# Two of the four weight sums of a seven-product matrix pair, added by DMAs that accumulate

## The chip, the cores and the metric

The kernel runs on one core of one Trainium2 chip. The metric is the device time of one execution in microseconds (us). The core has five instruction queues that work in parallel, each strictly in its own order: TensorE (PE in the profile; its weight loads are the row PEld), VectorE (DVE), ScalarE (ACT), GpSimd (POOL) and SyncE (SP, which here only issues DMAs). They wait for one another through semaphores. Sixteen DMA engines move data between the chip's memory (HBM) and the on-chip buffer (SBUF). A DMA can be issued from SP, as all weight loads of this kernel are, or from POOL.

## The reference

One transformer block on 512 tokens of width 1024: two kinds of attention, an output projection, and a gated feed-forward part of width 2816 with a short causal convolution, then a gated per-layer embedding. The change touches the first half of the feed-forward part alone:

```python
h = rmsnorm(x, mlp_pre_g[i])
gu = h @ w_gate_up[i]                  # [512, 1024] @ [1024, 2 * 2816]
a, u = jnp.split(gu, [D_FF], axis=-1)
a = causal_dwconv(a, conv_w[i], conv_b[i])
y = (gelu(a, approximate=True) * u) @ w_down[i]
```

All numbers are float32, and the kernel keeps that precision: each operand of a matmul is split into a high part, in the narrower format that TensorE takes at full rate (float32r), and a low part, the rest. One product is then three matmuls: high by high, low by high, high by low.

## The kernel before, in words

The 2816 columns of `a` and of `u` are cut into 22 tiles of 128. A *pair* j is tile j of `a` and tile j of `u`. Its weights come as two tiles of 128 partitions by 1024 numbers (512 KB each): `m[0]` (called `wr` in the profile, two buffers) for `a`, and `m[1]` for `u`. The 1024 numbers are the contraction's 8 chunks of 128 columns; `W` = 512 is half of them.

Pairs 0 to 8 are computed plainly. Pairs 9 to 21 (`SEVEN = range(9, NFF)`, 13 pairs) are computed as a product of 2 by 2 blocks in seven products in place of eight, in the manner of Strassen and Winograd. The blocks are the halves of the weights on one side, and on the other the halves of the contraction by the two halves of 256 tokens. This costs sums ahead of the products and behind them:

- `token_sums` makes sums and differences of the activations once, before the first such pair (`b` the blocks, `t` their four sums, all on DVE).
- `sums` makes four sums of the weights' halves for each pair, on DVE, 128x512 each. `s13` holds two of them: its left half is `m1[:, :W] + m1[:, W:]` (L1048), its right half `m0[:, :W] - m1[:, :W]` (L1056). `s24` holds the two that build on it (L1052, L1054).
- `high` and `low` split three operands of 128x1024 for each pair: `m0`, `s24` and `s13`. `high` is a copy on ACT (L1038), `low` a subtraction on DVE (L1042). `last_high` and `last_low` (L1060, L1064) do it for the right half of `m1`, 128x512.
- `product(j, n)` is 12 matmuls with 256 moving columns (lines L1080, L1083, L1084: four chunks, three matmuls each). Products 0 and 2 use the split `m0`, products 1 and 6 `s24`, 3 and 4 `s13`, 5 the right half of `m1`. A pair uses three PSUM banks `p[0]` to `p[2]`: products 0, 1, 3, 5 add up in `p[0]`, product 2 has `p[1]`, and 4 and 6 add up in `p[2]`.
- `evict(j, n)` takes what is in a bank out after product n, before the next product adds to it: n = 0, 1, 3 on ACT (L1091, L1094), n = 2, 4, 6 on DVE (L1096, L1098, L1100).
- `conv(j, n)` is the convolution and gelu (ACT L1114, DVE L1116 twice, ACT L1119); `finish` multiplies by `u` (DVE L1127 twice; L1129 for a plain pair).

The order of all this is written out by hand: `up_rest` puts each step into a list with a time (`at(t, f)`), sorts the list, and calls the steps; `keep` holds the instructions in that order on their engines. TensorE works two pairs interleaved: the products come in the order (j,0), (j-1,6), (j,1), (j,2), (j,3), (j,4), (j,5), (j+1,0), and so on. While TensorE multiplies for pair j, DVE and ACT prepare pair j+1. Between two instructions L1098 DVE therefore does, in this order: the four sums of the next pair but one, its `low` of `m0` and `last_low`, L1100, `low` of `s24`, L1116 twice, L1096, `low` of `s13`, L1127 twice, and the next L1098.

Buffers rotate by tag; what takes a buffer waits until the last reader of its former tenant is done. Tag `pt` has three: they hold `s13` and the low part of `s13` of the pairs in flight. Before the change the two tenants move round all three.

Of the kernel before, what the change touches and what calls it, by code (L numbers as in the profile page):

```python
# [8 lines left out]
F32 = mybir.dt.float32  # L9
F32R = mybir.dt.float32r  # L10
I32 = mybir.dt.int32
AF = mybir.ActivationFunctionType
ALU = mybir.AluOpType

P = 128
# [51 lines left out]
class Block:  # L67
# [909 lines left out]
    def token_sums(self):  # L977
# [6 lines left out]
        for p in range(Q):  # L984
# [7 lines left out]
            nc.vector.tensor_sub(t[:, 0:2, :], b[:, 1:4:2, :], b[:, 0:2, :])  # L992
            nc.vector.tensor_sub(t[:, 2, :], b[:, 3, :], t[:, 0, :])
            nc.vector.tensor_sub(t[:, 3, :], b[:, 2, :], t[:, 2, :])
# [11 lines left out]
    def up_rest(self, pending):  # L1006
# [20 lines left out]

        def load(j):
            w[j] = x = {"m": []}
            for i in range(2):  # L1030
                t = self.u([P, D], F32, "tt") if i else self.wrp.tile([P, D], F32, tag="wr", name=self.nm("wr"))
                keep(nc.sync.dma_start(t, io["gu"][2 * j + i]))
                x["m"].append(t)
# [10 lines left out]
        def sums(j, n):  # L1044
            m0, m1 = w[j]["m"]
            if n == 0:
                w[j]["s13"] = self.u([P, D], F32, "pt")
                keep(add(w[j]["s13"][:, :W], m1[:, :W], m1[:, W:]))  # L1048
            s13 = w[j]["s13"]
            if n == 1:  # L1050
                w[j]["s24"] = self.u([P, D], F32, "tt")
                keep(sub(w[j]["s24"][:, :W], s13[:, :W], m0[:, :W]))  # L1052
            if n == 2:
                keep(sub(w[j]["s24"][:, W:], m0[:, W:], w[j]["s24"][:, :W]))  # L1054
            if n == 3:
                keep(sub(s13[:, W:], m0[:, :W], m1[:, :W]))  # L1056

        def last_high(j):
            w[j]["x"] = x = self.u([P, 2, W], F32R, "wh")
            keep(act.activation(x[:, 0, :], w[j]["m"][1][:, W:], AF.Copy))  # L1060

        def last_low(j):
            x = w[j]["x"]
            keep(sub(x[:, 1, :], w[j]["m"][1][:, W:], x[:, 0, :].bitcast(F32)))  # L1064
# [56 lines left out]
        def finish(j):  # L1121
            z = st[j]
            y = self.y_room(j)
            if j in SEVEN:
                for i, u in enumerate((z["p"][0], z["e"][:, 1, :])):
                    t = slice(i * H, i * H + H)
                    keep(vec.tensor_mul(y[:, t], z["c"][:, t], u))  # L1127
# [13 lines left out]
        for j in js:  # L1141
            b = start[j] - (10.5 if j == NPLAIN else start[j] - start[j - 1])
            t = start[j]
            at(b - 7.0, lambda j=j: load(j))
            st[j] = {"p": []}
            if j in SEVEN:
                at(b - 1.0, lambda j=j: sums(j, 0))
                at(b - 0.4, lambda j=j: sums(j, 1))
                at(b + 0.2, lambda j=j: sums(j, 2))
                at(b + 0.8, lambda j=j: sums(j, 3))  # L1150
# [245 lines left out]
```

## Time and profile before

| | |
|---|---|
| Time, 3 runs | 665.62 us median (665.56 to 667.8) |
| Profiled execution | 668.27 us, of which the instructions span 666.5 us |
| Granted TensorE clock | 0.999 |
| PE busy over the span | 652.6 us (98%) |
| PEld busy | 565.5 us (85%) |
| DVE busy | 480.7 us (72%) |
| ACT busy | 363.1 us (54%) |
| POOL busy | 147.4 us (22%) |

The 1.8 us between span and time lie around the instructions. The shares are means over stages of different kinds. The seven-product pairs are the stage from about 362 us to 500 us after the span's start (the names `strassen_...`), where DVE and PE are both busy nearly all the time and POOL is idle. A row of the timeline gives an instruction's start, its duration, engine, line, operation and operands, and in brackets how long its engine had been idle before it and who ended that. The shown duration of a DVE or ACT instruction overlaps the next by about 0.1 us; from start to start is what it takes out of its queue. Rows with `x2` merge two like instructions. Of a DMA issue, the page gives the median time from issue to landing.

### The profile page before, as it was taken

The page shows a single profiled execution, that of the slowest core. Times are in us where ns is not written, and L with a number is a line of the kernel's source. Part 1 is how long each engine was busy: PE and PEld are TensorE (multiplying, and loading weights), DVE is VectorE, ACT ScalarE, POOL GpSimd, SP SyncE. Part 2 cuts the span into 40 slices and gives each one's busy share as a digit, 9 for nine tenths or more (in the row PEclk, how much of TensorE's full clock was granted, in tenths as well). Part 3 has the DMA queues.
Part 4 walks back from the last instruction along what each step waited for, and adds up shares of the span by engine and source line. Part 5 has one row for each costly group of instructions (what it writes and reads, how often), then busy time and mean ns, then how long its engine had stood idle before and what let it go on. Part 6 is the DMA issues. An engine that isn't in the chain of part 4 may idle for free.

```text
span 666.5 us, 10339 instructions
## 1 busy us (share of the span) xinstructions
PE 652.6 (98%) x3741; PEld 565.5 (85%) x3741; DVE 480.7 (72%) x965; ACT 363.1 (54%) x684; POOL 147.4 (22%) x223
## 2 busy tenths in 40 slices
PE   8999999999999999999999999999999999999996
PEld 7988768777888777888887999999998888889985
DVE  6795777878757757858999999999958333224872
ACT  6554688878868737445555565565736323222351
POOL 1021568558556241003221000000000000001000
PEclk9999999999999999999999999999999999999999
DMA  8346721111121557412241332332244554332031
GB/s 299 115 139 213 199 64 47 34 48 49 48 73 56 179 206 269 173 57 95 95 160 63 127 109 83 128 117 76 95 144 156 153 209 143 88 111 71 1 127 63
DMA packets 27282, 78.01 MB, mean 117 GB/s; under 512 B 3424, under 2 KB 4704, under 8 KB 27232
## 3 DMA queue, kind: packets, MB, share of 16 engines
q1 hardware_dynamic: 27088, 77.28, 35.6%
q8 instruction: 29, 0.48, 0.3%
q14 instruction: 21, 0.17, 0.1%
q10 hardware_dynamic: 144, 0.08, 0.0%
HBM read 63.72 MB, written 6.29 MB: 105 GB/s over the span
## 4 chain that ended last, share of the span: by engine, by line
PE 79%; DVE 11%; ACT 4%; DMA 2%; issue 2%; POOL 1%; ACTq 0%; DVEq 0%
PE nsa_pso L548 3%; PE mlpdown_pss L147 3%; PE mlpdown_pss L150 3%; PE mlpdown_pss L151 3%; PE strassen_pss L1080 3%; PE strassen_pss L1084 2%; PE strassen_pss L1083 2%; PE nsa_pst L515 2%; PE mlpdown_psmm L147 2%; PE mlpdown_psmm L150 2%; PE mlpdown_psmm L151 2%; DMA outproj_wr<-in_wo_dram 2%; PE strassen_pst L1080 2%; PE strassen_pst L1083 2%; PE strassen_pst L1084 2%
## 5 line engine op out<-in xcount | busy, mean ns | idle before, releaser
L132 DVE TENSOR_TENSOR mlpdown_wh<-mlpdown_wr,mlpdown_wh 128x1024 fp32r<-128x1024 f32 (+1 forms) x28 | 32.3, 1158 | 48.6 <-ACT mlpdown_wh L128 47.6
L128 ACT ACTIVATE mlpdown_wh<-mlpdown_wr 128x1024 fp32r<-128x1024 f32 (+1 forms) x28 | 27.9, 998 | 63.5 <-PE mlpdown_pss L150 25.9
L237 POOL TENSOR_TENSOR mlpdown_s<-mlpdown_s,mlpdown_s 128x512 f32<-128x512 f32 x6 | 7.8, 1292 | 238.1 <-ACT mlpdown_s L236 238.1
L537 POOL TENSOR_SCALAR nsa_u<-nsa_u,nsa_nrc,gate 128x512 f32<-128x512 f32 (+3 forms) x64 | 38.2, 607 | 22.5 <-DVE nsa_nrc L662 16.7
L1080 PE MATMUL strassen_pss<-sums_u,strassen_u 128*128 128x256 f32 x144 | 40.6, 282 | 1.6 <-ACT strassen_s L1091 1.6
L1084 PE MATMUL strassen_pss<-sums_u,strassen_u 128*128 128x256 f32 x144 | 40.5, 281 | 0.0
L1083 PE MATMUL strassen_pss<-sums_u,strassen_u 128*128 128x256 f32 x144 | 40.5, 281 | 0.0
L631 ACT ACTIVATE nsa_u<-nsa_u,nsa_nnm 128x512 f32<-128x512 f32 (+3 forms) x64 | 35.4, 555 | 5.3 <-DVE nsa_nnm L627 5.0
L519 DVE TENSOR_TENSOR nsa_u<-nsa_pst,nsa_u 128x512 fp32r<-128x512 f32 (+1 forms) x43 | 29.0, 684 | 9.1 <-ACT nsa_u L517 8.8
L627 DVE CUSTOM_DVE_ANT_0 nsa_u<-nsa_pss,biastables_u 128x512 f32<-128x512 f32 (+3 forms) x64 | 29.9, 485 | 5.4 <-PE nsa_pss L569 5.0
L1042 DVE TENSOR_TENSOR strassen_u<-strassen_u,strassen_u 128x1024 fp32r<-128x1024 f32 x27 | 33.3, 1237 | 0.0
L517 ACT ACTIVATE nsa_u<-nsa_pst 128x512 fp32r<-128x512 f32 (+1 forms) x43 | 25.1, 591 | 13.2 <-PE nsa_pst L515 12.8
L147 PE MATMUL mlpdown_pss<-mlpup_u,mlpdown_wh 128*128 128x512 f32 (+1 forms) x88 | 32.0, 364 | 0.0
L150 PE MATMUL mlpdown_pss<-mlpup_u,mlpdown_wh 128*128 128x512 f32 (+1 forms) x88 | 32.0, 364 | 0.0
L151 PE MATMUL mlpdown_pss<-mlpup_u,mlpdown_wh 128*128 128x512 f32 (+1 forms) x88 | 32.0, 363 | 0.0
L132 POOL TENSOR_TENSOR fill_wh<-fill_wr,fill_wh 128x512 fp32r<-128x512 f32 (+1 forms) x14 | 24.7, 1762 | 33.0 <-ACT fill_wh L128 32.9
L1038 ACT ACTIVATE strassen_u<-strassen_u 128x1024 fp32r<-128x1024 f32 x27 | 28.4, 1051 | 1.2 <-DVE strassen_u L1054 1.1
L1080 PEld LDWEIGHTS strassen_pss<-sums_u,strassen_u 128*128 128x128 f32 x144 | 27.3, 190 | 1.9 <-ACT strassen_s L1091 1.8
L548 PE MATMUL nsa_pso<-nsa_u,vnatural_u 128*128 128x512 f32 x72 | 27.2, 441 | 0.9 <-ACT nsa_u L517 0.3
L1083 PEld LDWEIGHTS strassen_pss<-sums_u,strassen_u 128*128 128x128 f32 x144 | 27.2, 189 | 0.1
L1084 PEld LDWEIGHTS strassen_pss<-sums_u,strassen_u 128*128 128x128 f32 x144 | 27.2, 189 | 0.0
L1083 PE MATMUL strassen_pst<-sums_u,strassen_u 128*128 128x256 f32 x88 | 24.8, 282 | 0.0
(502 smaller groups left out, 2302.9 us busy)
## 6 DMA issues: line engine op xcount, KB each, us to landing
mlpdown_wr<-in_down_dram SPq DMA_DIRECT2D x16, 512.0 KB, 3.6
strassen_wr<-in_gu_dram SPq DMA_DIRECT2D x14, 512.0 KB, 4.6
strassen_u<-in_gu_dram SPq DMA_DIRECT2D x14, 512.0 KB, 3.9
mlpup_wr<-in_gu_dram SPq DMA_DIRECT2D x10, 512.0 KB, 3.3
fill_wr<-in_win_dram SPq DMA_DIRECT2D x6, 512.0 KB, 3.8
mlpdown_wr<-in_down_dram SPq DMA_DIRECT2D x8, 384.0 KB, 3.2
fill_u<-fill_u SPq DMA_DIRECT2D x20, 128.0 KB, 2.5
loadx_u<-in_xT_dram SPq DMA_DIRECT2D x8, 256.0 KB, 4.7
```

What stands on the lines that cost most here:

```text
L132: l = eng.tensor_sub(lw, raw, hi.bitcast(F32))
L147: r = self.pin(mm(ps, hi, x[:, 0, :], start=start, stop=False))
L150: mm(ps, lo, x[:, 0, :], start=False, stop=False)
L151: mm(ps, hi, x[:, 1, :], start=False, stop=stop)
L537: self.nc.gpsimd.tensor_scalar(ap, ap, col, gate, op0=ALU.mult, op1=ALU.mult)
L548: self.att(nc.tensor.matmul(po, v, rhs, start=start, stop=stop))
L627: nc.vector.tensor_tensor_reduce(dst, src, dist, op0=ALU.add, op1=ALU.min, scale=SLOPES[8 + 4 * g + r], scalar=3e38, accum_out=nm[:, r, b ...
L631: nc.scalar.activation(dst, dst, AF.Exp, bias=nm[:, r, b : b + 1], scale=-1.0, accum_out=sm[:, r, b : b + 1])
L1042: keep(sub(lo, src, hi.bitcast(F32)))
L1080: r = mm(ps, hi[:, o], x[:, 0, :], start=fresh and p == 0, stop=False, skip_group_check=not fresh)
L1083: mm(ps, lo[:, o], x[:, 0, :], start=False, stop=False, skip_group_check=not fresh)
L1084: mm(ps, hi[:, o], x[:, 1, :], start=False, stop=p == Q - 1, skip_group_check=not fresh)
```

## The change

The sums in `s13` are made by DMAs. `load_sums(j)`, called 1.0 planned units ahead of `load(j)`, has SP load the left half of `m0` into the right half of `s13`, and the right half of `m1` into its left half. Then POOL issues one DMA that reads the left half of `m1` from HBM twice and adds it to both halves of `s13` in SBUF (`accum_op=ALU.add`). The left half of `m1` is no longer loaded by `load`, so `m[1]` of such a pair is 128x512.

A DMA can add but not subtract, so the signs move: the right half of `s13` is now `m0[:, :W] + m1[:, :W]`, the token sums `t` are formed with other signs (two of their four subtractions become scalar_tensor_tensor with a factor of -1), and `finish` multiplies by -1 as well (L1132, scalar_tensor_tensor in place of tensor_tensor). DVE's `sums` keeps two of its four instructions. The change is described as also treating one pair more in this way (14 of 22). The line `SEVEN = range(9, NFF)` stands in both kernels, though: 13 pairs before, 13 after.

```diff
@@ token_sums
-            nc.vector.tensor_sub(t[:, 0:2, :], b[:, 1:4:2, :], b[:, 0:2, :])
-            nc.vector.tensor_sub(t[:, 2, :], b[:, 3, :], t[:, 0, :])
-            nc.vector.tensor_sub(t[:, 3, :], b[:, 2, :], t[:, 2, :])
+            nc.vector.tensor_sub(t[:, 0:2, :], b[:, 0:4:3, :], b[:, 1:2, :].broadcast_to([P, 2, H]))
+            nc.vector.scalar_tensor_tensor(t[:, 2, :], b[:, 3, :], -1.0, t[:, 0, :], op0=ALU.mult, op1=ALU.subtract)
+            nc.vector.scalar_tensor_tensor(t[:, 3, :], t[:, 2, :], -1.0, b[:, 2, :], op0=ALU.mult, op1=ALU.subtract)
@@ up_rest
+        def load_sums(j):
+            w[j] = x = {}
+            x["s13"] = self.u([P, D], F32, "pt")
+            keep(nc.sync.dma_start(x["s13"][:, W:], io["gu"][2 * j][:, :W]))
+            keep(nc.sync.dma_start(x["s13"][:, :W], io["gu"][2 * j + 1][:, W:]))
+            keep(nc.gpsimd.dma_start(x["s13"].rearrange("p (b w) -> p b w", b=2),
+                                     io["gu"][2 * j + 1][:, None, :W].broadcast_to([P, 2, W]), accum_op=ALU.add))
+
         def load(j):
-            w[j] = x = {"m": []}
+            x = w.setdefault(j, {})
+            x["m"] = []
             for i in range(2):
                 t = self.u([P, D], F32, "tt") if i else self.wrp.tile([P, D], F32, tag="wr", name=self.nm("wr"))
-                keep(nc.sync.dma_start(t, io["gu"][2 * j + i]))
+                if i and j in SEVEN:
+                    t = t[:, W:]
+                keep(nc.sync.dma_start(t, io["gu"][2 * j + i][:, -t.shape[1] :]))
                 x["m"].append(t)
...
         def sums(j, n):
-            m0, m1 = w[j]["m"]
+            m0, s13 = w[j]["m"][0], w[j]["s13"]
             if n == 0:
-                w[j]["s13"] = self.u([P, D], F32, "pt")
-                keep(add(w[j]["s13"][:, :W], m1[:, :W], m1[:, W:]))
-            s13 = w[j]["s13"]
+                w[j]["s24"] = self.u([P, D], F32, "tt")
+                keep(add(w[j]["s24"][:, :W], s13[:, :W], m0[:, :W]))
             if n == 1:
-                w[j]["s24"] = self.u([P, D], F32, "tt")
-                keep(sub(w[j]["s24"][:, :W], s13[:, :W], m0[:, :W]))
-            if n == 2:
-                keep(sub(w[j]["s24"][:, W:], m0[:, W:], w[j]["s24"][:, :W]))
-            if n == 3:
-                keep(sub(s13[:, W:], m0[:, :W], m1[:, :W]))
+                keep(add(w[j]["s24"][:, W:], w[j]["s24"][:, :W], m0[:, W:]))
...
-                    keep(vec.tensor_mul(y[:, t], z["c"][:, t], u))
+                    keep(vec.scalar_tensor_tensor(y[:, t], u, -1.0, z["c"][:, t], op0=ALU.mult, op1=ALU.mult))
...
+            if j in SEVEN:
+                at(b - 8.0, lambda j=j: load_sums(j))
             at(b - 7.0, lambda j=j: load(j))
             st[j] = {"p": []}
             if j in SEVEN:
-                at(b - 1.0, lambda j=j: sums(j, 0))
-                at(b - 0.4, lambda j=j: sums(j, 1))
-                at(b + 0.2, lambda j=j: sums(j, 2))
-                at(b + 0.8, lambda j=j: sums(j, 3))
+                at(b + 0.2, lambda j=j: sums(j, 0))
+                at(b + 0.8, lambda j=j: sums(j, 1))
```

The orders of PE and ACT are the same before and after, instruction for instruction. From here on a line number above L1027 belongs to the kernel that the sentence speaks of; the new lines are L1033 (the accumulating DMA), L1031 and L1032 (its two loads), L1043 (`load`), L1053 (`low`), L1059 and L1061 (the two sums left), L1069 (`last_low`), L1101, L1103, L1105 (evictions 2, 4, 6), L1121 (convolution) and L1132 (`finish`).

On DVE, one pair's round before, from `low` of `s13` of one pair to the convolution. In brackets stand the queues that an instruction waits for: the engines' semaphores, `DMAHW` for DMAs of SP.

```order
L1042 TENSOR_TENSOR strassen_u_4212<-strassen_u_4133,strassen_u_4211 128x1024 [waits Activation_49]
L1127 TENSOR_TENSOR strassen_u_4117<-strassen_s_4194,strassen_pso_4009 128x256 [waits Activation_49]
L1127 TENSOR_TENSOR strassen_u_4117<-strassen_s_4194,strassen_s_4042 128x256
L1098 TENSOR_TENSOR strassen_s_4170<-strassen_s_4170,strassen_pss_4231 128x256 [waits PE_49,Activation_49]
L1048 TENSOR_TENSOR strassen_u_4260<-strassen_u_4192 128x512 [waits DMAHW5_49]
L1052 TENSOR_TENSOR strassen_u_4262<-strassen_u_4260,strassen_wr_4190 128x512 [waits DMAHW4_49,DVE_49]
L1054 TENSOR_TENSOR strassen_u_4262<-strassen_wr_4190,strassen_u_4262 128x512 [waits DVE_49]
L1056 TENSOR_TENSOR strassen_u_4260<-strassen_wr_4190,strassen_u_4192 128x512
L1042 TENSOR_TENSOR strassen_u_4279<-strassen_wr_4190,strassen_u_4278 128x1024 [waits Activation_49]
L1064 TENSOR_TENSOR strassen_u_4298<-strassen_u_4192,strassen_u_4298 128x512 [waits PE_49,Activation_49]
L1100 TENSOR_TENSOR mlpup_u_3149<-strassen_s_4170,strassen_pss_4231 128x256 [waits PE_49]
```

The same stretch now; `DMASW` stands for DMAs of POOL.

```order
L1053 TENSOR_TENSOR strassen_u_4220<-strassen_u_4048,strassen_u_4219 128x1024 [waits DMAHW0_49,PE_49,Activation_49]
L1132 SCALAR_TENSOR_TENSOR strassen_u_4124<-strassen_pso_4011,strassen_s_4202 128x256 [waits Activation_49]
L1132 SCALAR_TENSOR_TENSOR strassen_u_4124<-strassen_s_4045,strassen_s_4202 128x256
L1103 TENSOR_TENSOR strassen_s_4174<-strassen_s_4174,strassen_pss_4239 128x256 [waits PE_49,Activation_49]
L1059 TENSOR_TENSOR strassen_u_4281<-strassen_u_4177,strassen_wr_4198 128x512 [waits DMAHW6_49,DMAHW5_49,DMASW4_49]
L1061 TENSOR_TENSOR strassen_u_4281<-strassen_u_4281,strassen_wr_4198 128x512 [waits DVE_49]
L1053 TENSOR_TENSOR strassen_u_4284<-strassen_wr_4198,strassen_u_4283 128x1024 [waits Activation_49]
L1069 TENSOR_TENSOR strassen_u_4303<-strassen_u_4200,strassen_u_4303 128x512 [waits DMAHW7_49,PE_49,Activation_49]
L1105 TENSOR_TENSOR mlpup_u_3149<-strassen_s_4174,strassen_pss_4239 128x256 [waits PE_49]
```

Two instructions are gone, the first of the sums left waits for POOL's DMA, and `low` of `s13` (the first row) has got a wait for PE. It comes from the buffers: `s13` is now claimed a pair earlier, so that two of the three `pt` buffers always hold an `s13`, and every low part of `s13` is written to the third. That one is free when TensorE has read the former pair's low part for the last time, at the second-last matmul of product 4, the last but one of the matmuls that L1103 waits for.

On SP, the DMAs of the stage before: two of 512 KB for each pair, its `wr` (`m[0]`) and its `u` (`m[1]`). A `u` waits for DVE's `last_low` of the pair before, and with it the `wr` behind it.

```order
L1032 DMA strassen_u_4192<-in_gu_dram 128x1024 [waits DMAHW3_49,DVE_49]
L1032 DMA strassen_wr_4317<-in_gu_dram 128x1024 [waits DMAHW2_49]
L1032 DMA strassen_u_4319<-in_gu_dram 128x1024 [waits DMAHW5_49,DVE_49]
L1032 DMA strassen_wr_4445<-in_gu_dram 128x1024 [waits DMAHW4_49]
L1032 DMA strassen_u_4447<-in_gu_dram 128x1024 [waits DMAHW7_49,DVE_49]
```

And now: the two halves of `s13` (L1031, L1032) ahead of each `wr`. The wait for DVE of L1031 is for `low` of `s13` of the pair two before, whose buffer it takes.

```order
L1043 DMA strassen_u_4200<-in_gu_dram 128x512 [waits DMAHW3_49,DVE_49]
L1031 DMA strassen_u_4305<-in_gu_dram 128x512 [waits DMAHW0_49,DMAHW1_49,DMASW3_49,DVE_49]
L1032 DMA strassen_u_4305<-in_gu_dram 128x512
L1043 DMA strassen_wr_4326<-in_gu_dram 128x1024 [waits DMAHW2_49]
L1043 DMA strassen_u_4328<-in_gu_dram 128x512 [waits DMAHW7_49,DVE_49]
```

On POOL, which had one multiplication of this stage and then nothing until the next stage, the 13 accumulating DMAs now stand; here the first of them, among POOL's last work of the stage before.

```order
L974 TENSOR_TENSOR mlpup_s_3605<-mlpup_s_3605,r3b 128x512
L974 TENSOR_TENSOR mlpup_s_3695<-mlpup_s_3695,r3b 128x512
L1033 DMA strassen_u_3798<-in_gu_dram 128x2x512
L1144 TENSOR_TENSOR strassen_s_3811<-strassen_s_3811,r3b 128x512
L1033 DMA strassen_u_3858<-in_gu_dram 128x2x512
L1033 DMA strassen_u_3940<-in_gu_dram 128x2x512
```

The first accumulating DMA stands behind both L974 and ahead of the multiplication L1144, for which a `finish` on DVE waits; each of the DMAs waits for its two loads.

More of the change, by code (lines that the diff above doesn't have):

```diff
@@ L1044, in sums @@
         def sums(j, n):
-            m0, m1 = w[j]["m"]
+            m0, s13 = w[j]["m"][0], w[j]["s13"]
             if n == 0:
-                w[j]["s13"] = self.u([P, D], F32, "pt")
-                keep(add(w[j]["s13"][:, :W], m1[:, :W], m1[:, W:]))
-            s13 = w[j]["s13"]
+                w[j]["s24"] = self.u([P, D], F32, "tt")
+                keep(add(w[j]["s24"][:, :W], s13[:, :W], m0[:, :W]))
             if n == 1:
-                w[j]["s24"] = self.u([P, D], F32, "tt")
-                keep(sub(w[j]["s24"][:, :W], s13[:, :W], m0[:, :W]))
-            if n == 2:
-                keep(sub(w[j]["s24"][:, W:], m0[:, W:], w[j]["s24"][:, :W]))
-            if n == 3:
-                keep(sub(s13[:, W:], m0[:, :W], m1[:, :W]))
+                keep(add(w[j]["s24"][:, W:], w[j]["s24"][:, :W], m0[:, W:]))
         def last_high(j):
             w[j]["x"] = x = self.u([P, 2, W], F32R, "wh")
-            keep(act.activation(x[:, 0, :], w[j]["m"][1][:, W:], AF.Copy))
+            keep(act.activation(x[:, 0, :], w[j]["m"][1], AF.Copy))
         def last_low(j):
             x = w[j]["x"]
-            keep(sub(x[:, 1, :], w[j]["m"][1][:, W:], x[:, 0, :].bitcast(F32)))
+            keep(sub(x[:, 1, :], w[j]["m"][1], x[:, 0, :].bitcast(F32)))
         def product(j, n):
```

## The prediction, made before the changed kernel was run

> **What bounds the kernel now.** I read the page's busy times first, then the stages, then the waits of TensorE (PE) in the stage that is changed. The first line is from the page. The next three are busy time by stage (span, then each engine's busy time and instructions, granted clock, DMA share, GB/s), and the last is all that PE waited for between 300 and 480 us.
>
> ```profile
> PE 652.6 (98%) x3741; PEld 565.5 (85%) x3741; DVE 480.7 (72%) x965; ACT 363.1 (54%) x684; POOL 147.4 (22%) x223
> core 0: us, PE busy (x) PEld busy (x) DVE busy (x) ACT busy (x) POOL busy (x), PEclk, DMA share, GB/s
> 300.00:350.00 50.00, 50.00 (x222) 41.42 (x222) 45.27 (x66) 27.48 (x39) 13.98 (x7) 1.00 0.34 116
> 362.30:480.00 117.70, 116.06 (x977) 115.82 (x977) 114.95 (x176) 70.18 (x108) 0.00 (x0) 1.00 0.32 109
> PE strassen_pss L1080 <- ACT strassen_s L1091: 1.6, 1, 1.6
> ```
>
> In the stage, DVE is busy for 114.95 of 117.70 us, which looks like a bound. PE is busier still: 116.06, and it waited once, for 1.6 us, at the start. So no more than 1.6 us, a quarter of a percent, can come out of the waits here, however much DVE is relieved. PE sets the pace: 977 matmuls in 116.06 us are 0.1188 us each, 84 a pair, 9.98 us a pair.
>
> The next rows are DVE's timeline over one pair in the steady part; then PE's two last matmuls of a product 4 and the first of the product 3 that follows five products later; then two rows of ACT.
>
> ```profile
> 409.50 1.22 DVE L1042 TENSOR_TENSOR strassen_u<-strassen_u,strassen_u 128x1024 fp32r<-128x1024 f32 x1
> 410.64 0.41 DVE L1127 TENSOR_TENSOR strassen_u<-strassen_s,strassen_psmm 128x256 f32<-128x256 f32 x1
> 410.97 0.42 DVE L1127 TENSOR_TENSOR strassen_u<-strassen_s,strassen_s 128x256 f32<-128x256 f32 x1
> 411.45 0.42 DVE L1098 TENSOR_TENSOR strassen_s<-strassen_s,strassen_pss 128x256 f32<-128x256 f32 x1
> 411.79 0.68 DVE L1048 TENSOR_TENSOR strassen_u<-strassen_u 128x512 f32<-128x512 f32 x1
> 412.51 0.69 DVE L1052 TENSOR_TENSOR strassen_u<-strassen_u,strassen_wr 128x512 f32<-128x512 f32 x1
> 413.24 0.69 DVE L1054 TENSOR_TENSOR strassen_u<-strassen_wr,strassen_u 128x512 f32<-128x512 f32 x1
> 413.85 0.68 DVE L1056 TENSOR_TENSOR strassen_u<-strassen_wr,strassen_u 128x512 f32<-128x512 f32 x1
> 414.45 1.22 DVE L1042 TENSOR_TENSOR strassen_u<-strassen_wr,strassen_u 128x1024 fp32r<-128x1024 f32 x1
> 415.58 0.68 DVE L1064 TENSOR_TENSOR strassen_u<-strassen_u,strassen_u 128x512 fp32r<-128x512 f32 x1
> 416.19 0.41 DVE L1100 TENSOR_TENSOR mlpup_u<-strassen_s,strassen_pss 128x256 f32<-128x256 f32 x1
> 421.41 0.42 DVE L1098 TENSOR_TENSOR strassen_s<-strassen_s,strassen_psmm 128x256 f32<-128x256 f32 x1
> ...
> 410.95 0.28 PE L1083 MATMUL strassen_pss<-sums_u,strassen_u 128*128 128x256 f32 x1
> 411.07 0.28 PE L1084 MATMUL strassen_pss<-sums_u,strassen_u 128*128 128x256 f32 x1
> ...
> 418.30 0.28 PE L1080 MATMUL strassen_psmm<-sums_u,strassen_u 128*128 128x256 f32 x1
> ...
> 416.63 0.82 ACT L1114 ACTIVATE strassen_s<-mlpup_u,cols 128x512 f32<-128x512 f32 x1 [0.47 <-DVE mlpup_u L1100]
> 417.36 0.36 ACT L1094 ACTIVATE strassen_s<-strassen_psmm 128x256 f32<-128x256 f32 x1
> ```
>
> From L1098 to L1098 is 9.96 us, PE's pace. L1098 waits for the product that ends at 411.07 + 0.28 = 411.35 and starts 0.10 later; that hand-over is DVE's only idle time.
>
> **What DVE is spared.** L1048 takes 0.72 out of the queue (411.79 to 412.51), L1056 0.60. The two `finish` instructions turn into scalar_tensor_tensor; the row below has one of that size at 475 ns against 0.41 to 0.42 us, 0.06 more each. DVE gains 1.32 - 0.12 = 1.2 us a pair, over 13 pairs 15.6 us. Off the path: PE does not wait for it. Two of the 256-wide subtractions in each of four token sums lengthen likewise, 0.5 us in all, in a stage where PE is busy for 50.00 of 50.00.
>
> **The wait that `low` of `s13` gets.** Today it starts at 409.50. It will wait for PE's matmul of 410.95 (410.95 + 0.28 + 0.10 = 411.33), 1.8 us later, and all of DVE's queue stands behind it. From there, by the rows: 1.14 for itself, 0.39 for each L1132, 0.34 for L1103, so L1059 at 413.59; L1061 0.73 later, `low` of `m0` at 414.92, L1069 at 416.05, L1105 at 416.66 (L1100 stood at 416.19). ACT's L1119 follows 0.44 later, at 417.10, its next instruction, the eviction before product 3, at 417.83, and that ends at 418.19. PE wants it at 418.30. So the margin is 0.11 us, and a hand-over of about 0.1 eats it: I take 0, with up to 0.1 us a pair (1.2 us over 12) on the other side. L1103 ends at 413.67, and product 6, which needs its bank, begins two products after 411.19, at 414.04: covered. The spared 1.2 us become idle time ahead of this wait.
>
> **The DMAs.** SP issues the two loads when `low` of `s13` ends. In these rows, of DMA issues (median to landing), of SP's timeline and of groups of instructions, stand the prices.
>
> ```profile
> strassen_wr<-in_gu_dram SPq DMA_DIRECT2D x14, 512.0 KB, 4.6
> strassen_u<-in_gu_dram SPq DMA_DIRECT2D x14, 512.0 KB, 3.9
> mlpup_wr<-in_gu_dram SPq DMA_DIRECT2D x10, 512.0 KB, 3.3
> r_away<-pletiles_u SPq DMA_DIRECT2D x4, 512.0 KB, 6.0
> 416.30 0.33 SPq L1032 DMA_DIRECT2D strassen_u<-in_gu_dram  x1
> 416.68 0.43 SPq L1032 DMA_DIRECT2D strassen_wr<-in_gu_dram  x1
> L897 DVE SCALAR_TENSOR_TENSOR mlpdown_u<-mlpdown_u,cols,norm_pso 128x256 f32<-128x256 f32 x8 | 3.8, 475 | 0.0
> L237 POOL TENSOR_TENSOR mlpdown_s<-mlpdown_s,mlpdown_s 128x512 f32<-128x512 f32 x6 | 7.8, 1292 | 238.1 <-ACT mlpdown_s L236 238.1
> ```
>
> `low` lasts 1.22; SP reacts 0.04 after DVE (415.58 + 0.68 to 416.30); two halves together are the 512 KB that land in 3.9; a hand-over is 0.1. POOL can start 5.26 us after the start of `low`. L1059 of the next round asks for the result at 9.96 + 1.14 + 0.78 + 0.34 = 12.22. **The accumulating DMA may take 7.0 us** from POOL's start to its landing, call it D; beyond, DVE waits, and as the margin above is nil, PE does too.
>
> No DMA of POOL and none that adds is in this trace. Below, D is a plain load, 3.3. Above, it is a load and then a store of the same size, 3.9 + 6.0 = 9.9. In between I build it: 3.9 for the load; 1.1 for a second 512 KB to be read (the `wr` issued 0.38 behind the `u` lands 0.38 + 4.6 - 3.9 = 1.1 after it); 1.3 for POOL to write its descriptors, as much as an addition of 128x512 takes it (L237, 1292 ns). That is 6.3, under 7.0. The Trainium skill (Collectives: The Full Stack, The bandwidth ceiling: the fold count and why AG ≠ RS ≠ AR) says that an adding DMA is slower not for the addition but because it reads two sources: half the rate. By that, too, the second read is the surcharge; no run here shows it yet. Its page DMA: Bandwidth & Descriptors (Anatomy of one DMA — SWDGE (gpsimd) path) fits 2.0 us and the bytes at 436 GB/s, which for twice 512 KB estimates 4.4 us.
>
> Each pair moves 1792 KB in place of 1024; at a share of 0.32 now the engines have room. `wr` is issued earlier than today, `u` 0.4 us later but half the size.
>
> **The start.** Here rows of POOL, DVE and ACT around the first such pair.
>
> ```profile
> 346.84 2.56 POOL L974 TENSOR_TENSOR mlpup_s<-mlpup_s,r3b 128x512 f32<-128x512 f32 x1 [12.12 <-ACT mlpup_s L946]
> 354.69 1.74 POOL L1139 TENSOR_TENSOR strassen_s<-strassen_s,r3b 128x512 f32<-128x512 f32 x1 [5.29 <-ACT strassen_s L1119]
> ...
> 353.86 0.68 DVE L1048 TENSOR_TENSOR strassen_u<-strassen_u 128x512 f32<-128x512 f32 x1
> 355.30 1.67 DVE L1054 TENSOR_TENSOR strassen_u<-strassen_wr,strassen_u 128x512 f32<-128x512 f32 x1
> 356.90 0.68 DVE L1129 TENSOR_TENSOR strassen_u<-mlpup_pst,strassen_s 128x512 f32<-128x512 f32 x1
> 357.50 0.68 DVE L1056 TENSOR_TENSOR strassen_u<-strassen_wr,strassen_u 128x512 f32<-128x512 f32 x1
> ```
>
> The first accumulating DMA stands behind L974, so it starts at 349.40 and lands at 355.7 with D = 6.3. L1059 could run at 353.86, waits till 355.7, and is then where L1054 was, beside POOL's multiplication; the next `finish` needs that anyway. L1061 takes L1056's place at 357.5. Gain nothing. With D at 4.4 or less L1061 comes 0.4 earlier, as `finish` still waits for POOL until 356.43; with D = 8 it comes 1.1 later. Either goes straight into PE's one wait.
>
> **The sum**: start 0, steady part 0, so the profiled execution's 668.27 (span 666.5) stays, and the median is **665.6 us**; by itself this case holds 664.8 to 667.2.
>
> **Rivals.**
> - *The accumulating DMA is late* (slower; decides from D = 7.0). L1059 then sets the round, and since a buffer's two pairs form the circle, each us over costs half a us a pair: 11 pairs, 5.5 us. At 8.5, between 7.0 and 9.9: 665.6 + 8.2 = 673.8; at 9.9, 681.6. For: D is built of parts never seen together. Against: 0.7 us to spare.
> - *POOL hinders DVE.* L1054 took 1.67 in place of 0.69 while POOL multiplied. If writing descriptors does the same within the loop, 0.98 x 12 = 11.8: 677.4. Against: POOL starts 5.26 after `low`, when L1105 is just due (5.33), and what follows that has 1.3 us of slack. The Trainium skill (SBUF — State Buffer, Who interferes with whom) has two-input DVE instructions collide only with POOL work that reads SBUF, and takes it that descriptors only write; by that, this rival is empty. L1054's row agrees with the first half.
> - *PE runs faster* with less DVE traffic. Between 300 and 350 us 222 matmuls of 512 columns took 50.00 us, 0.1126 per 256; here it is 0.1188. All of it back would be 0.0062 x 1092 = 6.8 us: 658.8. Against: DVE was busy for 45.27 of those 50.00 too.
> - *It does not do what it says*: a fourteenth pair would save 48 x 0.2252 - 84 x 0.1188 = 0.8 us, but PE's order is unchanged, so it is not there.
>
> **Chances.** Forecast 0.62, late DMA 0.27 (of that 0.05 with D under 7.6, still within 0.5%, 3.3 us, about what a measurement of this kernel tells from no change), POOL 0.06, faster PE 0.05 (0.04 over 0.5%). Hence faster 0.04, same 0.68, slower 0.28. Range 663.5 to 675: it leaves out most of the faster case, and a late DMA with D over 8.7.
>
> **What would show it.** `low` of `s13` waiting for PE some 1.3 us each pair; L1059 not waiting for a DMA; L1094's successor before product 3 ending within 0.1 us of PE's need; PE still at 0.1188. Regular waits of PE for ACT ahead of product 3, with DVE waiting for POOL's DMA, make me wrong.

## The result, and the profile after

The changed kernel takes 672.0 us (median of 6, 669.98 to 673.15), the kernel before 666.4 beside it: 1.0079 of its time, 95% interval 1.0057 to 1.0102. I had forecast 665.6 and no change. The time lies in the range, but on the side of the first rival, the late accumulating DMA. In the profiled execution the span grew from 666.5 to 671.5 us.

Busy times of the changed kernel: the line of the page, then the same two stages as before (span, then busy time and instructions of PE, PEld, DVE, ACT, POOL; granted clock, DMA share, GB/s).

```profile
PE 654.3 (97%) x3741; PEld 565.8 (84%) x3741; DVE 463.7 (69%) x939; ACT 362.9 (54%) x684; POOL 162.9 (24%) x236
300.00:350.00 50.00, 50.00 (x222) 41.42 (x221) 45.52 (x66) 27.22 (x39) 14.58 (x8) 1.00 0.39 132
362.30:480.00 117.70, 114.11 (x947) 112.58 (x946) 94.31 (x144) 65.26 (x101) 13.39 (x11) 1.00 0.71 178
```

DVE did get its relief: 94.31 us in place of 114.95. PE issued 30 matmuls fewer in the same window, at a granted clock of 1.00 in both. So PE waited. The next rows are the first and the last 256-column matmul of the stage, first of the kernel before, then of the changed one.

```profile
362.34 0.28 PE L1080 MATMUL strassen_pss<-sums_u,strassen_u 128*128 128x256 f32 x1
499.48 0.28 PE L1084 MATMUL strassen_pss<-sums_u,strassen_u 128*128 128x256 f32 x1
```

```profile
362.07 0.28 PE L1085 MATMUL strassen_pss<-sums_u,strassen_u 128*128 128x256 f32 x1
504.80 0.28 PE L1089 MATMUL strassen_pss<-sums_u,strassen_u 128*128 128x256 f32 x1
```

The stage took 137.14 us and takes 142.73, which is 5.59 more: the whole loss, as the rest of the span is 0.6 shorter. Between waits the matmuls follow each other at 0.1186 us in both kernels, so nothing slows PE as such. All of it is waits.

What PE and DVE wait for in the loop of the changed kernel (total, times, longest):

```profile
PE strassen_pss L1085 <- ACT strassen_s L1096: 1.5, 1, 1.5
PE strassen_pss L1085 <- ACT strassen_s L1099: 1.4, 2, 1.0
PE strassen_pso L1085 <- ACT strassen_s L1099: 0.4, 1, 0.4
PE strassen_psmm L1085 <- ACT strassen_s L1099: 0.2, 1, 0.2
...
DVE strassen_u L1053 <- ACT strassen_s L1099: 12.3, 9, 1.5
DVE strassen_u L1059 <- DMA strassen_u<-in_gu_dram: 5.6, 8, 1.7
DVE strassen_u L1053 <- ACT strassen_u L1049: 4.0, 2, 2.1
```

The first row is the old wait at the start. The other waits of PE are new: ahead of product 3, for ACT's eviction L1099. The view puts them lower than they are; by the distance from one matmul to the next, less the usual 0.12, they sum to 5.8 us. In the same loop DVE's L1059 waits 5.6 us for a DMA. One us there is one us at PE, round by round: where L1059 is late by 0.49, 1.32 or 1.75 us, PE loses 0.51, 1.28 or 1.88.

The view puts the waits of `low`, L1053, down to ACT, for which it waits too. By the rows it starts 0.10 us after the end of PE's second-last matmul of product 4:

```profile
411.66 0.28 PE L1088 MATMUL strassen_pss<-sums_u,strassen_u 128*128 128x256 f32 x1
412.04 1.23 DVE L1053 TENSOR_TENSOR strassen_u<-strassen_u,strassen_u 128x1024 fp32r<-128x1024 f32 x1 [1.38 <-ACT strassen_s L1099]
```

So these are the waits for PE that the prediction foresaw, 16.3 us in eleven pairs, 1.5 us each.

One round in rows: `low` of `s13`, SP's loads, POOL's DMA, and the L1059 that reads its result; then the L1059 and the PE stall of the round before.

```profile
380.97 1.23 DVE L1053 TENSOR_TENSOR strassen_u<-strassen_u,strassen_u 128x1024 fp32r<-128x1024 f32 x1 [2.08 <-ACT strassen_u L1049]
382.23 0.33 SPq L1031 DMA_DIRECT2D strassen_u<-in_gu_dram  x1
382.61 0.44 SPq L1032 DMA_DIRECT2D strassen_u<-in_gu_dram  x1
387.07 1.21 POOL L1033 DMA_DIRECT2D strassen_u<-in_gu_dram  x1 [8.46 <-DVE strassen_u L1069]
394.33 0.69 DVE L1059 TENSOR_TENSOR strassen_u<-strassen_u,strassen_wr 128x512 f32<-128x512 f32 x1 [0.49 <-DMA strassen_u<-in_gu_dram]
...
383.81 0.69 DVE L1059 TENSOR_TENSOR strassen_u<-strassen_u,strassen_wr 128x512 f32<-128x512 f32 x1 [0.62 <-DMA strassen_u<-in_gu_dram]
386.89 0.42 DVE L1105 TENSOR_TENSOR mlpup_u<-strassen_s,strassen_pst 128x256 f32<-128x256 f32 x1
388.54 0.39 PE L1085 MATMUL strassen_pss<-sums_u,strassen_u 128*128 128x256 f32 x1 [0.38 <-ACT strassen_s L1099]
```

POOL starts 6.10 us after `low`, and the data are there 7.2 us after that: 13.3 in all, where the prediction had allowed 12.22. (The bracket of POOL's row names DVE; the second load landed at 382.61 + 3.8 = 386.41, 0.66 ahead of POOL.) The last three rows show how it reaches PE: L1059 0.62 late, L1105 behind it, then ACT, then PE, whose matmul comes 0.54 late.

### The profile page after: what moved, and what is told of

Same layout as the page of the kernel before. It is cut to its first block, busy times and chain, and to the rows that moved or that the text cites. A ratio compares the mean times of both kernels' runs of the same rounds, so it can differ in the third digit from the quotient of the medians.

```text
span 671.5 us, 10433 instructions
## 1 busy us (share of the span) xinstructions
PE 654.3 (97%) x3741; PEld 565.8 (84%) x3741; DVE 463.7 (69%) x939; ACT 362.9 (54%) x684; POOL 162.9 (24%) x236
## 4 chain that ended last, share of the span: by engine, by line
PE 64%; DVE 13%; DMA 12%; issue 5%; ACT 5%; POOL 1%; ACTq 0%; DVEq 0%; POOLq 0%
DMA strassen_u<-in_gu_dram 9%; PE nsa_pso L548 3%; DVE strassen_u L1053 3%; PE mlpdown_pss L147 3%; PE mlpdown_pss L150 3%; PE mlpdown_pss L151 3%; PE nsa_pst L515 2%; PE mlpdown_psmm L147 2%; PE mlpdown_psmm L150 2%; PE mlpdown_psmm L151 2%; DMA outproj_wr<-in_wo_dram 2%; PE mlpdown_pst L147 1%; PE mlpdown_pst L151 1%; PE mlpdown_pst L150 1%; PE fill_psmm L147 1%
## 5 line engine op out<-in xcount | busy, mean ns | idle before, releaser
L128 ACT ACTIVATE mlpdown_wh<-mlpdown_wr 128x1024 fp32r<-128x1024 f32 (+1 forms) x28 | 27.9, 998 | 63.6 <-PE mlpdown_pss L150 26.1
L1053 DVE TENSOR_TENSOR strassen_u<-strassen_u,strassen_u 128x1024 fp32r<-128x1024 f32 x27 | 33.4, 1240 | 16.3 <-ACT strassen_s L1099 12.3
L1033 POOL DMA_DIRECT2D strassen_u<-in_gu_dram x13 | 16.0, 1232 | 101.0 <-DVE strassen_u L1069 43.3
```

Of the source, the lines that this page charges most:

```text
L1053: keep(sub(lo, src, hi.bitcast(F32)))
```

## The experiments

All ratios are to the kernel before, run on the same chip, with 95% intervals. "Stage" is the time from the first to the last 256-column matmul, as above: 137.1 before, 142.7 with the change. "The loop" is the stage without its first wait.

**Without the accumulating DMA.**

```diff
-            keep(nc.gpsimd.dma_start(x["s13"].rearrange("p (b w) -> p b w", b=2),
-                                     io["gu"][2 * j + 1][:, None, :W].broadcast_to([P, 2, W]), accum_op=ALU.add))
```

> The accumulating DMA of L1033 is left out (so s13 holds the two raw halves, and the sums are not formed). Everything else of the change stays: the early claim of s13's buffer, the two loads of SP, the wait of low of s13 for PE, the two sums left to DVE. Theory A (the accumulating DMA lands too late for L1059): L1059 never waits for a DMA, since the second half lands about 4.1 us after the first is issued, 5.4 us after low's start against the 12.2 that are allowed; PE's stalls in the stage go from 5.7 us back to nothing, and the time is that of before, ratio 0.998 to 1.002. Theory B (the wait of low of s13 for PE, with the nil margin behind it, stretches the round by itself): the stalls stay, ratio 1.006 to 1.010.

0.9976 (0.9964 to 0.9989), stage 136.3. This is all PE waited for between 300 and 480 us:

```profile
PE strassen_pss L1083 <- ACT strassen_s L1094: 0.8, 1, 0.8
```

So the wait of `low` for PE costs nothing by itself; theory B falls. The first wait of the stage even shrank, from 1.6 to 0.8.

**A copying DMA in its place.**

```diff
-                                     io["gu"][2 * j + 1][:, None, :W].broadcast_to([P, 2, W]), accum_op=ALU.add))
+                                     io["gu"][2 * j + 1][:, None, :W].broadcast_to([P, 2, W])))
```

> The DMA of L1033 stays with its place, its queue, its 512 KB and its descriptors, but copies instead of adding (so the two loads before it are overwritten, and the sums are not formed). It prices the adding alone. Theory A with the surcharge that the prediction built (1.1 us for the second source): its time from POOL's start to landing falls from 6.1 to 8.4 (6.9 in the mean) to about 5.8, the DMA lands about 0.4 us before it is wanted, and the ratio is 0.999 to 1.003. If the adding costs nothing on top of the path through POOL's queue, that time stays near 6.9 and so does the ratio, 1.006 to 1.010. Theory C (POOL's writing of descriptors or the traffic as such hinders PE or DVE): ratio 1.006 to 1.010 even where L1059 no longer waits for a DMA.

0.9979 (0.9965 to 0.9993), stage 136.3, no wait of L1059 in the loop. The rows are POOL's group, the DMA's issue (KB, median us to landing) and POOL's DMA queue (packets, MB, share of the 16 engines), first with the copy, then with the addition.

```profile
L1033 POOL DMA_DIRECT2D strassen_u<-in_gu_dram x13 | 9.7, 744 | 102.0 <-DVE mlpup_u L1105 37.3
strassen_u<-in_gu_dram POOLq DMA_DIRECT2D x13, 512.0 KB, 4.8
q0 software_dynamic: 1872, 6.82, 3.0%
```

```profile
L1033 POOL DMA_DIRECT2D strassen_u<-in_gu_dram x13 | 16.0, 1232 | 101.0 <-DVE strassen_u L1069 43.3
strassen_u<-in_gu_dram POOLq DMA_DIRECT2D x13, 512.0 KB, 6.5
q0 software_dynamic: 3536, 6.82, 6.3%
```

The copy spares 0.5 us of POOL and 1.7 us to the landing; over the last ten rounds the means are 4.97 and 7.01, so 2.0. That is not the price of the adding alone, as I had meant it: the copy's descriptors are not those of the change. It moved its bytes in about half as many packets, 128 pieces a DMA in place of 256. The run with the row as it lies, below, parts the two. The same bytes over the same queue, copied, hinder nobody. The split further below, with all of the change's packets, hinders nobody either; so theory C falls too.

**A fourth buffer for `s13` and its low part.**

```diff
-SLOTS = {"u": 26, "kn": 4, "p": 6, "pt": 3, "tt": 2, "wh": 6}
+SLOTS = {"u": 25, "kn": 4, "p": 6, "pt": 4, "tt": 2, "wh": 6}
```

> The pool of s13 and its low part gets a fourth buffer (25 in place of 26 in the large pool), so that low of s13 no longer waits for PE, starts about 2 us earlier, and with it SP's loads and the accumulating DMA of two pairs later. The DMA itself stays as it is. Theory A: it lands about 1.4 us ahead of L1059 in the mean in place of 0.6 behind; at most one or two of the slowest (8.4 us) still make L1059 wait; ratio 0.998 to 1.003. Theory B: 0.998 to 1.002 as well. Theory C (traffic or descriptor writing): 1.006 to 1.010, as none of either is taken away.

0.9981 (0.9967 to 0.9994), stage 138.0. The time is as expected, the reason only in part:

```profile
DVE strassen_u L1059 <- DMA strassen_u<-in_gu_dram: 10.3, 10, 2.4
...
PE strassen_pss L1085 <- ACT strassen_s L1099: 0.5, 1, 0.5
```

L1059 waits even longer for the DMA than in the change, 10.3 us. But DVE is now ahead of PE, and only the largest of its waits come through (some 1.4 us by the distance of the matmuls, half of it in one round). The loads have become slower too: POOL starts 5.2 us after L1031 in place of 4.8. They overlap the accumulating DMA of the other pair for longer, 2.1 us in the mean in place of 1.2, which may be why. What the buffer bought was slack behind the DMA, not an earlier DMA.

**One of the two sums back on DVE.**

```diff
-            keep(nc.sync.dma_start(x["s13"][:, W:], io["gu"][2 * j][:, :W]))
...
-            keep(nc.gpsimd.dma_start(x["s13"].rearrange("p (b w) -> p b w", b=2),
-                                     io["gu"][2 * j + 1][:, None, :W].broadcast_to([P, 2, W]), accum_op=ALU.add))
+            keep(nc.gpsimd.dma_start(x["s13"][:, :W], io["gu"][2 * j + 1][:, :W], accum_op=ALU.add))
...
+            if n == 2:
+                keep(add(s13[:, W:], m0[:, :W], w[j]["m"][1][:, :W]))
```

> One of the two sums is added by the DMA (256 KB, the half that L1059 reads, behind one load of 256 KB), the other is back on DVE behind L1061 (0.6 us), so the second matrix is loaded whole again. Theory A: POOL starts some 0.4 to 1.0 us earlier, as it waits for one load, and the DMA of half the size takes 4.5 to 5.5 us: it lands 1.5 to 3 us before it is wanted; DVE's added 0.6 us pushes L1105 back, and by the nil margin behind it that would come through to PE at up to 0.6 us a pair unless low of m0 stays ahead of it. I expect ratio 1.000 to 1.004 with no DVE wait for a DMA; if there are stalls, they are in front of product 3 and every pair has one of the same size. Theory B: 1.006 or more.

1.0079 (1.0061 to 1.0098), stage 142.3: as slow as the change, and by another path. No wait for a DMA is left; the half DMA lands in 4.1 us. Instead each of ten rounds loses between 0.48 and 0.67 us ahead of product 3. Rows of one round (L1059 is the sum put back on DVE, L1103 DVE's last eviction):

```profile
401.63 1.23 DVE L1049 TENSOR_TENSOR strassen_u<-strassen_u,strassen_u 128x1024 fp32r<-128x1024 f32 x1 [1.40 <-PE strassen_pso L1086]
405.09 0.68 DVE L1059 TENSOR_TENSOR strassen_u<-strassen_wr,strassen_u 128x512 f32<-128x512 f32 x1
407.43 0.41 DVE L1103 TENSOR_TENSOR mlpup_u<-strassen_s,strassen_pso 128x256 f32<-128x256 f32 x1
408.60 0.36 ACT L1097 ACTIVATE strassen_s<-strassen_pst 128x256 f32<-128x256 f32 x1
```

From `low` of `s13` to the last eviction of DVE it is 5.80 us; without the extra sum it is 5.20 (rows of the split, below). That 0.60 costs some 0.53 a round. So the margin behind `low` is 0.07 us: the prediction had taken 0. The ratio that I expected, up to 1.004, had hoped that something ahead would absorb the sum; nothing does.

**The load of `wr` left out.**

```diff
+                if i == 0 and j > 11:
+                    x["m"].append(w[j - 2]["m"][0])
+                    continue
```

> The 512 KB load of wr, which SP issues right behind the two loads of s13, is left out from the fourth of the thirteen pairs on (these pairs go on using the first matrix of two pairs earlier, so their results are other numbers). Nothing else moves. It asks whether the accumulating DMA is late because other loads share the DMA engines with it and with the two loads ahead of it. If so: POOL starts 4.1 to 4.4 us after L1031 in place of 4.75, the DMA takes 6.1 to 6.4 in place of 6.9 in the mean, it lands about 0.4 us ahead of its need, and the ratio is 0.997 to 1.001. If the lateness is the path's own: POOL's start and the 6.9 stay within 0.2, L1059 goes on waiting, ratio 1.005 to 1.009.

1.0049 (1.0027 to 1.0070), stage 139.9, between the two answers. POOL starts 4.36 us after L1031 in place of 4.77, as the first answer has it. The DMA itself takes 6.3 to 7.7, 6.86 in the mean, as the second has it. So `wr` delays the two loads by 0.4, and the adding DMA is slow without it too. L1059 (L1062 in this run) still waited 2.8 us in the loop, and PE 3.0.

**The added row as it lies.**

```diff
-            keep(nc.gpsimd.dma_start(x["s13"].rearrange("p (b w) -> p b w", b=2),
-                                     io["gu"][2 * j + 1][:, None, :W].broadcast_to([P, 2, W]), accum_op=ALU.add))
+            keep(nc.gpsimd.dma_start(x["s13"], io["gu"][2 * j + 1], accum_op=ALU.add))
```

> The accumulating DMA adds the second matrix's row as it lies (128 pieces of 4 KB) in place of its left half twice (256 pieces of 2 KB); the bytes are the same, the sums are other numbers. If POOL's work and the DMA go by pieces: POOL's 1.22 us fall to about 0.9, the time to landing from 6.9 to under 6.2, and the ratio to 0.998 to 1.002. If they go by bytes: 6.6 to 6.9, ratio 1.004 to 1.009.

1.0023 (1.0006 to 1.0040), stage 138.5. POOL's part fell from 1.22 to 0.88, and POOL's start to landing from 7.01 to 6.13 in the mean (5.3 to 7.6). So pieces of 4 KB in place of 2 KB save 0.9 us at equal bytes, over a third of it in POOL: the first answer. L1059 (L1058 in this run) waited 1.5 us in the loop, PE 1.8. POOL's queue:

```profile
q0 software_dynamic: 1872, 6.82, 6.3%
```

These are the packets and bytes of the copy, and yet the engines are busy with them for 6.3% of the span in place of 3.0%. So the adding doubles the engines' time, whatever the pieces: an estimate from these shares, the spans and 13 DMAs is about 3.2 us of all sixteen engines a DMA against 1.5. To the landing it costs 6.13 - 4.97 = 1.2 us, and the pieces of 2 KB the other 0.9 of the 2.0. (The copy reads 2 KB twice where this DMA reads 4 KB; I take that to cost nothing.)

**The same DMA twice.**

```diff
+            for _ in range(2):
```

> The accumulating DMA is issued twice, the second behind the landing of the first (so the left half is added twice to each sum, other numbers). This lengthens the path by some 7.3 us (0.6 hand-over and 6.7). Theory A with the prediction's price, half a us a pair for each us of lateness, since the circle spans two pairs: 0.6 to 0.7 late becomes 8, 4.0 us a pair, 11 pairs, 44 us: ratio 1.055 to 1.075. If each us of lateness cost a whole us a pair: ratio 1.12 to 1.14. If PE absorbs it elsewhere: under 1.04.

1.118 (1.114 to 1.122), some 78 us: far more than the 44 of my price, and at the edge of what a whole us per us was to cost. The rounds tell more than the sum. From `low` to L1060 (L1059 in the change) it is 20.6 us in this one, 8.4 over:

```profile
383.45 1.23 DVE L1054 TENSOR_TENSOR strassen_u<-strassen_u,strassen_u 128x1024 fp32r<-128x1024 f32 x1 [3.58 <-issue]
404.09 0.69 DVE L1060 TENSOR_TENSOR strassen_u<-strassen_u,strassen_wr 128x512 f32<-128x512 f32 x1 [3.11 <-DMA strassen_u<-in_gu_dram]
```

Half of it makes rounds of 9.97 + 4.2 = 14.2 us, all of it 18.4. Over nine rounds L1031 is issued every 15.4. What comes on top of the half goes with the clock of the stage (same columns as at the head):

```profile
362.30:480.00 117.70, 90.86 (x596) 89.14 (x597) 63.53 (x93) 45.81 (x69) 18.22 (x15) 0.80 0.68 152
```

PE is granted 0.80 of its clock here, against 1.00 in the change. After most of its long waits the matmuls come every 0.21 us instead of 0.12 for a while. By the distances of the matmuls, PE waits for 45 us in the loop, some 7.5 us at the stage's start, and loses another 26 us to matmuls at the slower pace. So the waits are about the 44 us of my price, and most of what comes on top is the clock. The parting is not exact, since a slower PE stretches the rounds and hides some waiting.

**The DMA split in two, the half that L1059 reads first.**

```diff
-            keep(nc.sync.dma_start(x["s13"][:, W:], io["gu"][2 * j][:, :W]))
-            keep(nc.sync.dma_start(x["s13"][:, :W], io["gu"][2 * j + 1][:, W:]))
-            keep(nc.gpsimd.dma_start(x["s13"].rearrange("p (b w) -> p b w", b=2),
-                                     io["gu"][2 * j + 1][:, None, :W].broadcast_to([P, 2, W]), accum_op=ALU.add))
+            for o, r, c in ((slice(0, W), 2 * j + 1, slice(W, D)), (slice(W, D), 2 * j, slice(0, W))):
+                keep(nc.sync.dma_start(x["s13"][:, o], io["gu"][r][:, c]))
+                keep(nc.gpsimd.dma_start(x["s13"][:, o], io["gu"][2 * j + 1][:, :W], accum_op=ALU.add))
```

> The accumulating DMA is split in two of 256 KB, each issued as soon as the load of its own half has landed, and the half that L1059 reads goes first; three buffers as in the change, and the whole computation. Theory A: as with the one half that was added by DMA (POOL 3.3 us behind SP's load, 4.1 to landing), the first half lands about 8.7 us after the start of low, 3.5 us ahead of L1059; the second lands some 12 us after it, and nothing wants it before the high part of s13, 4.5 us behind L1059. No DVE wait for a DMA, no PE stall inside the loop, ratio 0.996 to 1.001, as where nothing was added. Theory B or C: 1.006 to 1.010.

0.9972 (0.9959 to 0.9985), stage 136.3. This is the whole computation, with the change's three buffers and its relief of DVE, and it is 2.8 parts in a thousand faster than the kernel before. One of its twelve executions took 1651 us; it is not in the ratio, and I do not know why. PE's waits between 300 and 480 us:

```profile
PE strassen_pss L1084 <- ACT strassen_s L1095: 0.8, 1, 0.8
```

The issues of POOL's DMAs between 362.3 and 480 us:

```profile
strassen_u<-in_gu_dram POOLq DMA_DIRECT2D x22, 256.0 KB, 6.2
```

DVE in one round, from `low` to the last eviction (L1058 is L1059 in the change):

```profile
418.23 1.22 DVE L1052 TENSOR_TENSOR strassen_u<-strassen_u,strassen_u 128x1024 fp32r<-128x1024 f32 x1 [1.42 <-ACT strassen_s L1098]
420.37 0.68 DVE L1058 TENSOR_TENSOR strassen_u<-strassen_u,strassen_wr 128x512 f32<-128x512 f32 x1
423.43 0.42 DVE L1104 TENSOR_TENSOR mlpup_u<-strassen_s,strassen_psmm 128x256 f32<-128x256 f32 x1
```

L1058 starts 2.14 us after `low` and waits for nothing. My 4.1 for each half was wrong: that is what one takes alone, two in flight take 6.2 in the median. It is early all the same, because POOL need not wait for the second load: it begins 3.6 us in the mean after the first load is issued, in place of 4.8. What the profiles show of the gain is the first wait of the stage: 1.80 us there by the distance of its matmuls, 0.92 here, as in the two runs without an addition. That is 0.9 of the 1.9 us that the ratio says; its interval begins at 1.0. The rest is not shown to be the split's. The fastest executions of the two kernels differ by 0.8 us (664.45 and 665.26), and the two profiled ones are 1.9 us apart already at the first matmul of `compress` (24.2 and 26.1 us into the span), in a part that no edit touches.

**One more pair by seven products, on top of the split.**

```diff
-SEVEN = range(9, NFF)
+SEVEN = range(8, NFF)
```

> The split version with one more of the pairs done by seven products (all 14 of the stage, the plain one at its start too). By the prediction's price a seven-product pair saves 48 x 0.2252 - 84 x 0.1188 = 0.8 us of PE, so 0.8 us under the split version, ratio 0.995 to 0.997 of before, if the sums of that pair and its accumulating DMA find room in the mlp-up stage ahead, where DVE is busy for 18.78 of 20 us. If they do not, PE waits at the start of the stage for the first sums, by 1.5 us or more, and the ratio is 0.999 or above.

1.0187 (1.0166 to 1.0208). The second answer, far above its floor: these are PE's waits from 340 to 480 us, and then two stretches at the stage's start.

```profile
PE strassen_pss L1084 <- ACT strassen_s L1095: 5.1, 1, 5.1
PE strassen_pss L1087 <- DVE strassen_u L1052: 3.5, 1, 3.5
```

```profile
350.00:360.00 10.00, 4.04 (x18) 3.24 (x17) 7.33 (x10) 3.38 (x4) 1.88 (x3) 0.76 0.71 129
360.00:370.00 10.00, 7.33 (x39) 7.33 (x40) 5.93 (x9) 4.80 (x8) 3.07 (x3) 0.56 0.69 183
```

PE waits 3.5 us for a `low` of the added pair, which stands behind the last work on the token sums and a wait of 1.7 us for POOL's DMA, and 5.1 us for ACT's first eviction, which stands behind the gelu of the plain pair and a `high`. In the two stretches it runs at a granted clock of 0.76 and 0.56. In this order, at least, there is no room for one more pair's work at the end of the mlp-up stage.

**The change once more.** It is the kernel of the change, unaltered.

> The changed kernel itself once more, beside the same runs of the kernel before as the version above, so that their ratios can be set against each other. Theory A expects what it showed: ratio 1.006 to 1.010, PE's stalls in the loop equal in sum to what L1059 waits for the DMA from the second pair on (5.7 against 5.6 us in the first execution), and each round's lateness that of its own DMA.

1.0092 (1.0064 to 1.0120), stage 143.7. L1059 waited 4.6 us in the loop and PE 4.8. Another 1.5 us went to a slower clock right after the first wait of the stage (last section).

## Why the prediction was wrong

*What bounds the kernel; what DVE is spared.* Right. PE's pace stayed at 0.119 us. In the split version, whose rounds are as short as before, DVE is busy for 99.98 us between 362.3 and 480, 15.0 less than before or 1.27 a round, and it bought nothing in the loop. The two `finish` instructions were not dearer (0.41 to 0.42, as before), so that surcharge of 0.06 was not there.

*The wait of `low` for PE, and the margin behind it.* Right. `low` waits 1.5 us a pair where 1.3 were foretold; without the accumulating DMA PE never waits in the loop. The margin was taken as nil, up to 0.11; the extra 0.60 us on DVE put it at 0.07.

*The DMAs.* **Here it failed, in two terms of the sum.** First, "POOL can start 5.26 us after the start of `low`" was 6.0 in the mean. The second load is issued 0.38 us after the first and lands 3.7 after that, so 4.1 in place of 3.9, and POOL begins some 0.6 to 0.7 after the landing in place of my 0.1; behind a single load that landed in 2.7 it also began only after 3.3. 0.4 us of the landing is `wr`, which is queued right behind. Second, "That is 6.3, under 7.0" was 7.01 in the mean of the last ten rounds (6.2 to 8.4): just what I had allowed, with nothing left for the first error. Of its three parts, the load and POOL's descriptors, 3.9 + 1.3 = 5.2, were right as a sum (4.97 for the copy, though POOL's part of that is 0.72), and so was 1.1 for the second source: the addition cost 1.2 at equal packets. What the sum put at nothing, without a reason, is that the DMA goes in 256 pieces of 2 KB; that made 0.9. So 13.0 us stood against 12.22. Either error alone would have left the DMA at most 0.1 us late (6.02 + 6.3 = 12.32, 5.26 + 7.01 = 12.27).

*The price.* Right as a rate. The table has means over the last ten rounds. Of each sum I take what exceeds 12.22, and half of that on 9.97 gives the expected round; the last column is the mean distance of L1031's issues.

| kernel | `low` to POOL | POOL to landing | expected round | measured |
|---|---|---|---|---|
| the change | 6.02 | 7.01 | 10.37 | 10.37 |
| the change again | 6.06 | 6.91 | 10.34 | 10.34 |
| without `wr` | 5.61 | 6.86 | 10.09 | 10.20 |
| the row as it lies | 5.94 | 6.13 | 9.97 | 10.02 |
| a copy | 5.78 | 4.97 | 9.97 | 9.97 |

Close to the bound the half is too little, since a round that is early gives nothing back for one that is late; taken round by round, the rule gives 10.12 without `wr` and 10.05 for the row as it lies, still short of the 10.20. The last round is worst: its DMA took 8.4 us and L1059 waited 1.75. It falls together with the first weights of the next stage; whether they are the cause was not tried.

*The start.* "Gain nothing" held for the change as built (1.80 us before, 1.62 and 1.93 after). The gain that the prediction named for a short DMA, 0.4 us, came where L1059 waited for none, as 0.9 us.

*Rivals.* The first was what happened, with 0.27 given to it, and what the prediction named as its refutation is what the trace shows: PE waits for ACT ahead of product 3, and DVE for POOL's DMA. Its D of 8.5 was too high, but it had left the loads out. That POOL hinders DVE showed nowhere: in the split POOL is busy for 19.53 us between 362.3 and 480, and DVE's rows there keep their 0.41, 0.69 and 1.22 us. That PE runs faster did not show either.

*The rules weighed.* The Trainium skill (Collectives: The Full Stack, The bandwidth ceiling: the fold count and why AG ≠ RS ≠ AR) has the adding step of a collective at half the rate of a copy, since it reads two sources. The trace agrees: 6.3% against 3.0% of the engines' time for the same packets and bytes. To the landing it is less, 6.13 us against 4.97. The Trainium skill (DMA: Bandwidth & Descriptors, Anatomy of one DMA — SWDGE (gpsimd) path) has a fit of 2.0 us and the bytes at 436 GB/s; by it an estimate is 3.2 us for the copy, where this stage shows 4.1 to 6.0, and 4.4 for twice the bytes, where the addition takes 6.1 to 8.4. Here the measurement decides, and every one of these values lies above the fit.

What stays open is why the same DMA takes 6.2 us in one round and 7.8 in another. Leaving out `wr` did not narrow it. Nor is it known why POOL begins only 0.6 to 0.7 us after a load has landed.

## What to carry to other kernels

A DMA that takes work from an engine puts its whole latency into the loop that recycles its buffer: add up issue, landing, the reaction of the queue that waits, and the DMA itself with the pieces that it goes in, and do not call 0.7 us of slack enough when two of these terms were never seen in that place. Where a reader needs only one half of what a DMA delivers, split it and send that half first; here this took away the loss of 0.8% and left the kernel 0.3% under the one before, about half of which the traces show. And when an engine is spared, look at the margin behind its new wait: with 0.07 us there, every 0.6 us put back on DVE cost 0.5 on PE, while the 1.3 us a round that were taken off it were worth nothing.

## What the runs showed of the hardware that I had not expected

An accumulating DMA of 512 KB keeps POOL for 1.22 us and lands after 6.1 to 8.4; a copying one of the same shape 0.72 and 4.1 to 6.0; an accumulating one of 256 KB 0.88 and 4.1 when alone, 6.2 with its twin. Adding takes the DMA engines 2.1 times as long as copying the same bytes in the same packets (6.3% against 3.0% of the span).

A short wait can cost PE its clock. In the second run of the change the first wait of the stage leaves 2.05 us between two matmuls, 1.93 over the usual distance. The rows are PE's timeline, then a window of the stages view:

```profile
363.26 0.28 PE L1089 MATMUL strassen_pss<-sums_u,strassen_u 128*128 128x256 f32 x1
365.31 0.39 PE L1085 MATMUL strassen_pss<-sums_u,strassen_u 128*128 128x256 f32 x1 [1.77 <-ACT strassen_s L1096]
365.54 0.28 PE L1088 MATMUL strassen_pss<-sums_u,strassen_u 128*128 128x256 f32 x1
...
366.24 0.41 PE L1085 MATMUL strassen_pss<-sums_u,strassen_u 128*128 128x256 f32 x1
366.46 0.41 PE L1088 MATMUL strassen_pss<-sums_u,strassen_u 128*128 128x256 f32 x1
```

```profile
365.20:368.50 3.30, 3.19 (x17) 3.19 (x18) 3.27 (x5) 2.38 (x5) 1.21 (x1) 0.62 0.37 151
```

From 365.89 on the matmuls come every 0.21 us for 3.4 us, at a granted clock of 0.62 over the window of the last row (its last column but two), and PE loses 1.5 us on top of the wait. Waits of 1.62 and 1.80 us at the same place, in the change's first execution and in the kernel before, left the clock at 1.00. In the run with the DMA twice a wait of 1.93 us at 549 us was followed by 3.4 us at the same slow pace. The Trainium skill (TensorE: Matmul & The Clock Gate, HAM oscillation — how this bites in real kernels) warns of gaps in PE's work of over some 3.4 us; a gap of about 2 was enough in this run.
